# Reordering the work between the sub-layers of a two-layer diffusion trunk: where partial sums are taken, where conditioning products stand, which engine scales the first row

## The chip, the cores and the metric

The kernel runs on one core of a Trainium2 chip. The metric is device time in microseconds of one execution. The kernel before takes 1449.47 us (median of 3 runs, 1449.01 to 1450.84). All times in this text are microseconds unless marked otherwise.

A core has a matrix engine (PE, whose weight loads are listed as PEld), a vector engine (DVE), an activation engine (ACT), a general engine (POOL) and a queue engine that issues transfers (SP). Each runs its own instruction stream in order, and they wait for each other through semaphores.

## The reference

Two layers over 128 context tokens and 256 latent tokens of width 1024. Each layer has two sub-layers, a mixer and a convolutional feed-forward network, and each sub-layer has the same frame:

```python
for layer in range(2):
    mod = silu(cond) @ mod_w[layer] + mod_b[layer]          # six vectors of 1024, for context and for latents
    h = rmsnorm(x, w_pre) * (1 + mod[1]) + mod[0]           # pre-norm, shift and scale
    o = mixer(h)                                            # layer 0: SSD + DeltaNet; layer 1: gating MLP + attention
    x = x + mod[2] * rmsnorm(o, w_post)                     # post-norm, gate, residual
    h = rmsnorm(x, w_pre2) * (1 + mod[4]) + mod[3]
    o = (silu(a) * b) @ w_down                              # a, b = split(conv3(h @ w_up))
    x = x + mod[5] * rmsnorm(o, w_post2)
```

So between two sub-layers stands a serial stretch: the last output tile of `o` gives a sum of squares over 1024 features per token, its inverse root scales `o`, that updates `x`, a second inverse root scales `x`, and only then can the first matmul of the next sub-layer start. There are three such stretches inside the kernel and one at its end.

## The kernel before

**Layout.** Features lie on the 128 partitions, in 8 rows of tiles; tokens lie along the free axis (386 columns: 128 context tokens, a gap of 2, 256 latent tokens). A projection takes a 128x1024 block of weights per output tile. The weights come as 32-bit floats and are split into a high part (`whi`, a cast on ACT, L345) and a low part (`wlo`, a subtraction on DVE, L348); activations are split in the same way (`hh`, L371; `hl`, L372). Every product is three matmuls of 386 columns: high by high, low by high, high by low.

**Weights in order.** `plan` holds the list of all weight blocks. `fetch` takes the next one: a transfer of 512 KB from SP into one of 3 `wst` buffers (L339), then the split of its two halves of 512 columns into 6 `whi` and 6 `wlo` buffers. `wload` keeps two blocks ahead.

**Conditioning products.** `mod` is computed in 12 quads per layer (`quad`). A quad is five steps: four steps that each bring 512 KB of `mod_w` (L297) and do 8 small products on PE (L301; the profile counts 16 instructions for them, since each runs as two passes), and a fifth that copies the result on ACT (L305), transposes it on PE (L308) and adds the bias on DVE (L310). Its accumulator is one of the four PSUM buffers that the projections use too. Quads are placed in three ways: mixed one by one into the fill of a mixer (`weave`, with the quads' weights in the `wst` buffers), one step per index of the feed-forward network's loop (`early`, the constant `Q5`), or by `step(n)` between two sub-layers. The constants `S0`, `S1`, `S2` say how many steps are taken at three places there, by stretch (`gap` 0 after the layer 0 mixer, 1 after the layer 0 network, 2 after the layer 1 mixer). `Q2` and `Q4` say where the quads mixed into a mixer's fill end and those beside a residual begin. What is left is drained after the next pre-norm.

**Between two sub-layers.** `residual` takes the 8 output tiles. For each it squares the tile (L513), scales it into `u` by the gate (L508), squares that (L516) and multiplies it by `x` (L517): three partial products, added up over the tiles in `acc` (L520: the first on DVE, the two others on POOL). `colsum` (L498) turns such a tile into per-token means with three products of a single column (six instructions). In the kernel before, tiles 0 to 5 of the first sum and tile 6 of it are taken by `before`, called inside the last tile; the two other sums are taken after the last tile. Then `rsq` (an add on DVE, L409 or L411, and a power on POOL, L412) and `spread` (L420, six instructions on PE) give `r` and, by way of four small DVE instructions on `q` (L544 to L411), `r2`. After that `prenorms` goes through the 8 rows: `update` (`u*r` on DVE, L563; `x += u` on POOL, L564), `x*r2` on DVE (L471), shift and scale on ACT (L473, one instruction for context and one for latents), then the split into `hh` and `hl`. The first matmul group of the next sub-layer (`group`, L393 and L395) takes three output tiles at once, row by row, 9 matmuls per row.

**Order.** A scheduler that the kernel's language provides draws up each engine's stream at compile time, by the order of the program and by its own estimates of when an instruction is ready; a `with issue_after(ins)` block makes the instructions traced inside it follow `ins` on the engine of `ins`, and adds no wait between engines.

Of the kernel before, what the change touches and what calls it, by code (L numbers as in the profile page):

```python
# [27 lines left out]
S0, S1, S2 = [1, 2, 2], [9, 8, 4], [0, 0, 0]  # L28
# [207 lines left out]
class Net:  # L236
# [55 lines left out]
    def quad(self, l, q, pool):  # L292
        nc = self.nc
        acc = self.pmm.tile([128, 256], F32, name="pmod", tag="mm")
        for j in range(4):
            w = pool.tile([128, 1024], F32, name="wmod", tag="wst" if pool is self.wst else "wmod")
            nc.sync.dma_start(out=w, in_=self.t[f"modw_l{l}"][4 * q + j])  # L297
            for k in (2 * j, 2 * j + 1):
                for c in range(4):
                    o = 512 * (k % 2) + 128 * c  # L300
                    nc.tensor.matmul(acc[32 * c:32 * c + 32, 0:128], self.cond[:, k, :], w[:, o:o + 128],  # L301
                                     start=(k == 0), stop=(k == 7), tile_position=(0, 32 * c))
# [22 lines left out]
    def plan(self, seq):  # L325
        self.seq, self.ready, self.help, self.gap = list(seq), [], False, -1
# [8 lines left out]
    def fetch(self, after):  # L335
# [4 lines left out]
        parts = []  # L340
        for o in range(0, n, 512):
            m = min(512, n - o)
            hi, lo = (self.spare(n) or p.tile([128, 512], F32R, name=n, tag=n) for n, p in (("whi", self.whi), ("wlo", self.wlo)))
            with self.follow(after and after[0]):
                self.conv_hi = nc.scalar.copy(out=hi[:, 0:m], in_=st[:, o:o + m])  # L345
            eng = nc.gpsimd if o and self.help else nc.vector
            with self.follow(after and after[1]):
                self.conv_lo = eng.tensor_sub(out=lo[:, 0:m], in0=st[:, o:o + m], in1=hi[:, 0:m].bitcast(F32))  # L348
            parts.append((hi, lo))
        self.ready.append((src, parts))  # L350
# [9 lines left out]
    def prefetch(self, n, after=None):  # L360
        while len(self.ready) < n and self.seq:
            self.fetch(after)
# [7 lines left out]
    def split(self, hi, lo, src, eng=None):  # L370
        self.nc.scalar.copy(out=hi, in_=src)  # L371
        (eng or self.nc.vector).tensor_sub(out=lo, in0=src, in1=hi.bitcast(F32))  # L372
# [79 lines left out]
    def prenorms(self, l, nm, slot, r, hp, update=None, mods=None):  # L452
# [7 lines left out]
        step = 8 if mods is None else 2  # L460
        for k in range(8):
# [14 lines left out]
            if update:  # L476
# [1325 lines left out]
```

## Time and profile before

| | us |
|---|---|
| median of 3 runs | 1449.47 |
| the profiled execution's own time | 1449.51 |
| its span, first to last instruction | 1447.7 |
| PE busy | 1379.6 (95%) |
| DVE busy | 956.8 (66%) |
| ACT busy | 792.7 (55%) |
| POOL busy | 198.4 (14%) |

The span is what the views of the trace show; 1.8 us lie around it. PE is counted busy where a matmul is under way, and matmuls overlap, so busy time is not time at full rate. The profile also lists the clock that PE was granted, as a share of 2.4 GHz: 1.00, or 0.50 for 1.2 GHz, and a number between the two for a stretch that holds both.

### The profile page before, as it was taken

Reading aid. Unit: us, or ns where it says so; the run is one execution under the profiler, and the core shown is the slowest. Engines: PE = TensorE matmul, PEld = TensorE weight load, DVE = VectorE, ACT = ScalarE, POOL = GpSimd, SP = SyncE. Lnnn points to the kernel's source line nnn. Section 1 sums busy time; section 2 is a strip of 40 time slices with the busy share of each in tenths; the row PEclk is TensorE's granted clock in tenths of the full one; section 3 lists DMA queues with packets and bytes.
Section 4 is the critical chain, followed back from the end, with each engine's and each line's share of the span. In section 5 each row is a group of like instructions: output and inputs, shape, how many; then the busy total and the mean of one; then the engine's idle time right before and its main releaser. Section 6 shows DMA issues by size and latency. Waiting matters only on the chain.

```text
span 1447.7 us, 26153 instructions
## 1 busy us (share of the span) xinstructions
PE 1379.6 (95%) x10133; PEld 1306.4 (90%) x10133; DVE 956.8 (66%) x1879; ACT 792.7 (55%) x1749; POOL 198.4 (14%) x186
## 2 busy tenths in 40 slices
PE   5999998999998999999999999999999999999996
PEld 3889887999987789899999998999999899999996
DVE  3586999855989766676666445566567486767432
ACT  3578665668585436555455444544855465555341
POOL 0023110012355304200000113000002300000001
PEclk9999999999999999899999999999999999999998
DMA  9334544412643474545543442544234334343441
GB/s 347 130 101 142 174 138 143 142 42 79 199 161 117 139 238 170 210 154 162 170 134 114 128 126 74 160 146 134 83 117 153 125 117 131 117 131 115 128 126 55
DMA packets 60332, 201.58 MB, mean 139 GB/s; under 512 B 7120, under 2 KB 12000, under 8 KB 60208
## 3 DMA queue, kind: packets, MB, share of 16 engines
q1 hardware_dynamic: 52832, 186.25, 40.1%
q10 hardware_dynamic: 6048, 8.93, 1.7%
q0 software_dynamic: 1328, 4.73, 1.1%
q8 instruction: 80, 1.31, 0.4%
q14 instruction: 44, 0.36, 0.1%
HBM read 191.20 MB, written 8.68 MB: 138 GB/s over the span
## 4 chain that ended last, share of the span: by engine, by line
PE 79%; DVE 11%; issue 3%; ACT 3%; POOL 3%; DMA 1%; POOLq 0%; SPq 0%; ACTq 0%; DVEq 0%
PE mm L393 19%; PE mm L378 11%; PE mm L379 11%; PE mm L380 11%; PE mm L395 9%; PE pmod L301 3%; DVE wlo L348 2%; PE ps L498 1%; DVE t L700 1%; PE ps L1625 1%; PE mmt L1550 1%; PE mmt L1551 1%; PE mmt L1552 1%; DVE er L1133 1%; POOL er L809 1%
## 5 line engine op out<-in xcount | busy, mean ns | idle before, releaser
L348 DVE TENSOR_TENSOR wlo<-wst,whi 128x512 fp32r<-128x512 f32 (+1 forms) x497 | 344.2, 699 | 189.0 <-ACT whi L345 185.0
L345 ACT CAST whi<-wst 128x512 fp32r<-128x512 f32 (+1 forms) x505 | 304.2, 612 | 282.9 <-PE mm L379 151.2
L393 PE MATMUL mm<-hh,whi 128*128 128x386 f32 x728 | 247.7, 340 | 5.8 <-ACT hh L371 4.9
L393 PE MATMUL mm<-hh,wlo 128*128 128x386 f32 x728 | 245.9, 338 | 0.0
L395 PE MATMUL mm<-hl,whi 128*128 128x386 f32 x728 | 239.6, 340 | 0.3
L378 PE MATMUL mm<-hh,whi 128*128 128x386 f32 x552 | 198.0, 359 | 4.7 <-ACT t L1341 2.8
L380 PE MATMUL mm<-hh,wlo 128*128 128x386 f32 x552 | 191.6, 347 | 0.6 <-DVE wlo L348 0.6
L379 PE MATMUL mm<-hl,whi 128*128 128x386 f32 x552 | 191.9, 348 | 0.0
L393 PEld LDWEIGHTS mm<-hh,whi 128*128 128x128 f32 x728 | 137.1, 188 | 8.6 <-ACT hh L371 5.8
L395 PEld LDWEIGHTS mm<-hl,whi 128*128 128x128 f32 x728 | 136.1, 188 | 1.5 <-DVE hl L372 1.4
L393 PEld LDWEIGHTS mm<-hh,wlo 128*128 128x128 f32 x728 | 137.3, 189 | 0.0
L378 PE MATMUL mm<-gh,whi 128*128 128x386 f32 x352 | 119.5, 339 | 0.0
L379 PE MATMUL mm<-gl,whi 128*128 128x386 f32 x352 | 119.2, 339 | 0.0
L380 PE MATMUL mm<-gh,wlo 128*128 128x386 f32 x352 | 118.9, 338 | 0.0
L378 PEld LDWEIGHTS mm<-hh,whi 128*128 128x128 f32 x552 | 107.5, 195 | 11.9 <-issue 6.1
L598 DVE SCALAR_TENSOR_TENSOR t<-mm,vecs,t 128x385 f32<-128x385 f32 x88 | 54.3, 618 | 87.1 <-ACT t L597 87.1
L379 PEld LDWEIGHTS mm<-hl,whi 128*128 128x128 f32 x552 | 107.4, 195 | 0.7 <-issue 0.2
L380 PEld LDWEIGHTS mm<-hh,wlo 128*128 128x128 f32 x552 | 106.5, 193 | 1.0 <-DVE wlo L348 0.9
L700 DVE SCALAR_TENSOR_TENSOR t<-mm,vecs,t 128x384 f32<-128x384 f32 (+1 forms) x152 | 92.7, 613 | 12.3 <-ACT t L694 8.1
L597 ACT ACTIVATE t<-mm,vecs 128x386 f32<-128x386 f32 x88 | 58.9, 674 | 72.4 <-PE mm L395 72.4
L520 POOL TENSOR_TENSOR sums<-sums,t 128x386 f32<-128x386 f32 x36 | 41.5, 1175 | 337.6 <-DVE t L517 281.4
L301 PE MATMUL pmod<-wmod,cond 128*32 128x128 f32 x1536 | 67.2, 297 | 0.3 <-issue 0.3
(423 smaller groups left out, 2589.9 us busy)
## 6 DMA issues: line engine op xcount, KB each, us to landing
wmod<-modw_l SPq DMA_DIRECT2D x96, 512.0 KB, 4.4
wst<-up_l SPq DMA_DIRECT2D x88, 512.0 KB, 3.5
wst<-w SPq DMA_DIRECT2D x56, 512.0 KB, 4.0
wst<-wo SPq DMA_DIRECT2D x32, 512.0 KB, 3.9
wst<-down_l SPq DMA_DIRECT2D x32, 512.0 KB, 3.6
wst<-w1f SPq DMA_DIRECT2D x18, 512.0 KB, 3.6
wst<-down_l SPq DMA_DIRECT2D x16, 384.0 KB, 3.2
wst<-w1t SPq DMA_DIRECT2D x10, 512.0 KB, 3.6
```

The source lines that it names most:

```text
L301: nc.tensor.matmul(acc[32 * c:32 * c + 32, 0:128], self.cond[:, k, :], w[:, o:o + 128], start=(k == 0), stop=(k == 7), tile_position=(0, 3 ...
L345: self.conv_hi = nc.scalar.copy(out=hi[:, 0:m], in_=st[:, o:o + m])
L348: self.conv_lo = eng.tensor_sub(out=lo[:, 0:m], in0=st[:, o:o + m], in1=hi[:, 0:m].bitcast(F32))
L378: mm(ps, wh, xh, start=start, stop=False)
L379: mm(ps, wh, xl, start=False, stop=False)
L380: return mm(ps, wl, xh, start=False, stop=stop)
L393: mm(ps, w[k // 4][p][:, s], hh[:, k, :], start=(k == 0 and p == 0), stop=False)
L395: mm(ps, w[k // 4][0][:, s], hl[:, k, :], start=False, stop=(k == 7))
L520: (nc.gpsimd if i else v).tensor_add(out=acc[:, i, :], in0=acc[:, i, :], in1=p)
L597: nc.scalar.activation(out=cv, in_=ps, func=AF.Identity, scale=cw(1), bias=self.v(f"ffb_l{l}", n))
L598: stt(out=cv[:, 1:T], in0=ps[:, 0:T - 1], scalar=cw(0), in1=cv[:, 1:T], op0=ALU.mult, op1=ALU.add)
L700: nc.vector.scalar_tensor_tensor(out=o, in0=p, scalar=cw(i), in1=o, op0=ALU.mult, op1=ALU.add)
```

## The change

- `before` takes all three sums of `acc` inside the last tile. Tile 6 is added to `acc` for all three sums in stretches 1 and 2 (and for the one sum of the last residual); in stretch 0 (`direct`) tile 6 is not added at all, its products go to `colsum` one by one. `before` is called earlier in the last tile of both feed-forward networks (from row 16 to row 14 of 22) and of the layer 0 mixer (from row 5 to row 4 of 8), and later in that of the layer 1 mixer (from the start of its second half to the middle of it).
- The next weight block is fetched, and its first half split, right after the last tile; its second half is split behind the `hh` cast and the `hl` subtraction of row 0. Before, both halves followed the square of tile 7 (on ACT) and the first root (on DVE).
- Conditioning steps: one before the sum of tile 7's squares, two behind the last sum (`hold`), one behind `r2`: 4 in each stretch, where there were 10, 10 and 6. In exchange quad 1 of layer 1 moves into the layer 0 mixer's fill (`Q2`), six more steps into the layer 0 network's loop (`Q5`), and quad 10 into the layer 1 mixer's fill (`Q4`). `quad` now yields its fourth step before the ACT copy.
- Row 0: `x += u` moves from POOL to DVE, and the latents' shift and scale move from ACT to DVE (`first`). `x*r2` of rows 1 to 7 and `u*r` of rows 2 to 7 are queued behind `first` on DVE.

```diff
-S0, S1, S2 = [1, 2, 2], [9, 8, 4], [0, 0, 0]
+S0, S1, S2 = [1, 1, 1], [2, 2, 2], [1, 1, 1]
...
+            with self.follow(self.hold):
+                for k in (2 * j, 2 * j + 1):
...
-            if j == 3:
-                s = self.t386()[:, 0:128]
-                nc.scalar.copy(out=s, in_=acc[:, 0:128])
             yield 0.45
+        s = self.t386()[:, 0:128]
+        nc.scalar.copy(out=s, in_=acc[:, 0:128])
...
+        self.rest = self.halves(st, n, parts)
+        if halves:
+            next(self.rest)
+        else:
+            drain(self.rest)
...
             if update:
-                update(k)
-            nc.vector.tensor_mul(out=h, in0=self.x[:, k, :], in1=r)
+                with self.follow(first and k > 1 and first.ins):
+                    update(k)
+            with self.follow(first and first.ins):
+                nc.vector.tensor_mul(out=h, in0=self.x[:, k, :], in1=r)
             for s, (b, e) in enumerate(SEGS):
+                if update and k == 0 and s:
+                    first = nc.vector.tensor_scalar(out=h[:, b:e], in0=h[:, b:e], scalar1=a[:, k, s:s + 1],
+                                                    scalar2=m[:, k, 0, s:s + 1], op0=ALU.mult, op1=ALU.add)
+                    continue
...
-            self.split(hh[:, k, :], hl[:, k, :], h)
+            cast, cut = self.split(hh[:, k, :], hl[:, k, :], h)
+            if update and k == 0:
+                with self.follow(cast.ins), self.follow(cut.ins):
+                    drain(self.rest)
...
+        direct = self.gap == 0
+
         def before():
-            colsum(0, acc[:, 0, :], True)
-            colsum(0, part[0], False)
+            for i in range(num):
+                colsum(i, acc[:, i, :], i == 0)
+            if direct:
+                colsum(0, part[0], False)
...
-            if n:
-                for i, p in list(enumerate(part))[n // 6:]:
+            if 0 < n < 7 - direct:
+                for i, p in enumerate(part):
...
         o = out_tile(7, before)
+        if not last:
+            self.fetch(1)
+        if direct:
+            colsum(2, six[2], False)
...
-            colsum(2, acc[:, 2, :], True)
+            self.step(S0[self.gap])
         colsum(0, part[0], False)
...
-            colsum(1, acc[:, 1, :], True)
+            if direct:
+                colsum(1, six[1], False)
...
-            self.step(S0[self.gap])
+            self.hold = tail.ins
+            self.step(S2[self.gap])
             r2 = self.spread(rt2)
             self.step(S1[self.gap])
-            self.prefetch(3, (sq.ins, self.roots[0]))
+            self.hold = None
...
-                eng.tensor_add(out=self.x[:, n, :], in0=self.x[:, n, :], in1=u[:, n, :])
+                (eng if n else v).tensor_add(out=self.x[:, n, :], in0=self.x[:, n, :], in1=u[:, n, :])
...
-                    if mid and k0 + k == 16:
+                    if mid and k0 + k == 14:
...
-Q2 = 1
+Q2 = 2
 Q0 = 0
 Q3 = 8
-Q4 = 10
-Q5 = 15
+Q4 = 11
+Q5 = 21
...
-                if mid and k == 5:
+                if mid and k == 4:
...
+                w = net.wload(src(n, i))
+                half(ps, w, i, *x, range(4))
                 if mid and i:
                     mid()
-                half(ps, net.wload(src(n, i)), i, *x)
+                half(ps, w, i, *x, range(4, 8))
```

(Of S1 and S2 the roles change too: `S2` was a number of steps per row of the pre-norm, and now is the number taken behind the last sum.)

## Rows read from the trace of the kernel before

**Rows 1.** The page, busy time of PE: us, share, instructions.

```profile
PE 1379.6 (95%) x10133; PEld 1306.4 (90%) x10133; DVE 956.8 (66%) x1879; ACT 792.7 (55%) x1749; POOL 198.4 (14%) x186
```

**Rows 2.** Windows by stage: window, length, busy time by engine, PE clock, DMA share.

```profile
569.30:574.59 5.29, 4.10 (x23) 3.57 (x22) 2.81 (x4) 2.44 (x6) 3.54 (x4) 0.81 0.44 161
574.59:593.75 19.16, 17.07 (x172) 14.57 (x172) 6.82 (x21) 5.14 (x14) 6.10 (x7) 0.61 0.52 182
...
884.16:897.86 13.70, 11.38 (x172) 9.48 (x172) 6.80 (x21) 5.22 (x14) 6.04 (x6) 0.88 0.14 40
897.86:911.27 13.41, 13.28 (x74) 12.87 (x75) 10.10 (x19) 10.49 (x24) 4.97 (x6) 1.00 0.22 64
1136.96:1150.83 13.87, 11.73 (x155) 9.69 (x154) 5.84 (x17) 4.98 (x13) 4.58 (x5) 0.75 0.52 190
1150.83:1166.09 15.26, 14.06 (x89) 13.03 (x90) 12.69 (x23) 11.25 (x25) 6.45 (x7) 1.00 0.04 9
```

**Rows 3.** Timeline of PE, stretch 1: start, length, engine, line, operands, count, idle before.

```profile
885.97 1.50 PE L301 MATMUL pmod<-wmod,cond 128*32 128x128 f32 x42
887.40 0.83 PE L498 MATMUL ps<-cst,sums 128*128 128x1 f32 x6
888.09 1.48 PE L498 MATMUL ps<-cst,t 128*128 128x1 f32 x12
889.43 1.09 PE L420 MATMUL ps<-cst,rsq 128*128 128x130 f32 x6
...
891.80 1.65 PE L420 MATMUL ps<-cst,rsq 128*128 128x130 f32 x6 [0.29 <-POOL rsq L412]
...
897.86 0.44 PE L393 MATMUL mm<-hh,whi 128*128 128x386 f32 x1 [1.65 <-ACT hh L371]
```

**Rows 4.** Timeline of DVE, stretch 1.

```profile
885.47 0.62 DVE L530 TENSOR_TENSOR t<-mm,t 128x128 f32<-128x128 f32 x2 [4.63 <-ACT t L508]
...
889.68 0.16 DVE L544 TENSOR_TENSOR q<-ps,rsq 128x3 f32<-128x3 f32 x1 [3.44 <-PE ps L498]
...
890.34 0.69 DVE L348 TENSOR_TENSOR wlo<-wst,whi 128x512 fp32r<-128x512 f32 x1
...
891.63 0.55 DVE L563 TENSOR_TENSOR u<-u,ps 128x386 f32<-128x386 f32 x1
893.66 0.17 DVE L310 TENSOR_TENSOR mod<-pmod,vecs 128x8 f32<-128x8 f32 x1 [1.49 <-PE pmod L308]
893.74 1.48 DVE L563 TENSOR_TENSOR u<-u,ps 128x386 f32<-128x386 f32 x3
895.14 0.55 DVE L471 TENSOR_TENSOR t<-xres,ps 128x386 f32<-128x386 f32 x1
```

**Rows 5.** Timeline of ACT, stretch 1.

```profile
884.25 0.49 ACT L526 ACTIVATE t<-mm 128x386 f32<-128x386 f32 x1 [4.13 <-PE mm L380]
...
895.79 1.61 ACT L473 ACTIVATE t<-t,mod,ma 128x128 f32<-128x128 f32 x3
897.31 0.50 ACT L371 CAST hh<-t 128x386 fp32r<-128x386 f32 x1
```

**Rows 6.** Timeline of POOL, stretch 1.

```profile
890.50 1.24 POOL L412 TENSOR_TENSOR rsq<-rsq,mhalf 128x3 f32<-128x3 f32 x1 [3.33 <-DVE rsq L411]
892.25 1.00 POOL L564 TENSOR_TENSOR xres<-xres,u 128x386 f32<-128x386 f32 x1 [0.51 <-DVE u L563]
```

**Rows 7.** Windows of both networks' up halves, conditioning products (L301) alone: PE, PEld busy.

```profile
593.75:789.40 195.65, 7.11 (x192) 4.69 (x192) 1.00 0.48 153
1150.83:1339.90 189.07, 0.65 (x16) 0.38 (x16) 1.00 0.38 118
```

**Rows 8.** Timeline of PE, last tile of the layer 0 mixer.

```profile
571.22 0.83 PE L498 MATMUL ps<-cst,t 128*128 128x1 f32 x6 [1.19 <-ACT t L513]
```

**Rows 9.** Timeline of POOL, the same tile: two of the sums of tile 5.

```profile
568.30 2.70 POOL L520 TENSOR_TENSOR sums<-sums,t 128x386 f32<-128x386 f32 x2 [0.32 <-ACT t L516]
```

**Rows 10.** Timeline of PE, first matmul group after stretch 2: the transpose of a quad.

```profile
1162.61 0.33 PE L308 MATMUL pmod<-cst,t 128*128 128x128 f32 x1 [1.14 <-ACT t L305]
```

More of the change, by code (lines that the diff above doesn't have):

```diff
@@ L297, in quad @@
             nc.sync.dma_start(out=w, in_=self.t[f"modw_l{l}"][4 * q + j])
[L298 to L302, printed above, removed]
-            if j == 3:
-                s = self.t386()[:, 0:128]
-                nc.scalar.copy(out=s, in_=acc[:, 0:128])
+            with self.follow(self.hold):
+                for k in (2 * j, 2 * j + 1):
+                    for c in range(4):
+                        o = 512 * (k % 2) + 128 * c
+                        nc.tensor.matmul(acc[32 * c:32 * c + 32, 0:128], self.cond[:, k, :], w[:, o:o + 128],
+                                         start=(k == 0), stop=(k == 7), tile_position=(0, 32 * c))
             yield 0.45
+        s = self.t386()[:, 0:128]
+        nc.scalar.copy(out=s, in_=acc[:, 0:128])
         tr = acc[:, 128:256]
@@ L325, in plan @@
     def plan(self, seq):
-        self.seq, self.ready, self.help, self.gap = list(seq), [], False, -1
+        self.seq, self.ready, self.help, self.gap, self.hold = list(seq), [], False, -1, None
         self.more = {"whi": 0, "wlo": 0}
@@ L333, in spare, with fetch @@
         return self.extra.tile([128, 512], F32R, name=name, tag=name, bufs=MORE)
-    def fetch(self, after):
+    def fetch(self, halves=0):
         nc = self.nc
@@ L340, in fetch, with halves @@
         parts = []
+        self.ready.append((src, parts))
+        self.rest = self.halves(st, n, parts)
[3 more added lines that the diff above has]
+            drain(self.rest)
+    def halves(self, st, n, parts):
+        nc = self.nc
         for o in range(0, n, 512):
@@ L343, in fetch @@
             hi, lo = (self.spare(n) or p.tile([128, 512], F32R, name=n, tag=n) for n, p in (("whi", self.whi), ("wlo", self.wlo)))
-            with self.follow(after and after[0]):
-                self.conv_hi = nc.scalar.copy(out=hi[:, 0:m], in_=st[:, o:o + m])
+            self.conv_hi = nc.scalar.copy(out=hi[:, 0:m], in_=st[:, o:o + m])
             eng = nc.gpsimd if o and self.help else nc.vector
-            with self.follow(after and after[1]):
-                self.conv_lo = eng.tensor_sub(out=lo[:, 0:m], in0=st[:, o:o + m], in1=hi[:, 0:m].bitcast(F32))
+            self.conv_lo = eng.tensor_sub(out=lo[:, 0:m], in0=st[:, o:o + m], in1=hi[:, 0:m].bitcast(F32))
             parts.append((hi, lo))
-        self.ready.append((src, parts))
+            yield
     @contextmanager
@@ L358, in follow, with prefetch @@
         return self.tc.issue_after(ins) if ins else nullcontext()
-    def prefetch(self, n, after=None):
+    def prefetch(self, n):
         while len(self.ready) < n and self.seq:
-            self.fetch(after)
+            self.fetch()
     def wload(self, src, ahead=2):
@@ L370, in split @@
     def split(self, hi, lo, src, eng=None):
-        self.nc.scalar.copy(out=hi, in_=src)
-        (eng or self.nc.vector).tensor_sub(out=lo, in0=src, in1=hi.bitcast(F32))
+        return (self.nc.scalar.copy(out=hi, in_=src),
+                (eng or self.nc.vector).tensor_sub(out=lo, in0=src, in1=hi.bitcast(F32)))
     def acc(self, ps, w, k, xh, xl, start, stop):
@@ L460, in prenorms @@
         step = 8 if mods is None else 2
+        first = None
         for k in range(8):
@@ L523, in residual @@
             scaled(gx, self.x[:, 7, :], 7, AF.Copy)
+        six = part
         o = out_tile(7, before)
+        if not last:
+            self.fetch(1)
+        if direct:
+            colsum(2, six[2], False)
         part = [self.t386() for i in range(num)]
```

2 lines of the change are left out of this document (removed).

## The prediction

> **What bounds the kernel now.** I read the page first. PE is busy 95% of the span [rows 1], so most stages are bound by PE, and an edit pays only where PE waits or does something that need not be on the path. Then the windows by stage: the three stretches between sub-layers, from the end of the last tile's last matmul to the first matmul of the next group, take 19.16, 13.70 and 13.87, and the clock granted in them is 0.61, 0.88 and 0.75, while it is 1.00 in the matmul groups behind them [rows 2]. That is 46.7 in sum in which no projection runs. Last the timelines of stretch 1, engine by engine, which show what its 13.70 consist of:
>
> - PE does 42 conditioning instructions (885.97) before it takes the 18 instructions of the sums that `q` needs (887.40 to 889.43); `q` starts at 889.68, late by those 42 [rows 3, 4].
> - The power on POOL takes 1.24, the spread of `r2` 1.65 and ends at 893.45 [rows 3, 6].
> - `x*r2` of row 0 could start there, but starts at 895.14: ahead of it on DVE stand two halves of `wlo`, the bias of a quad, which waits 1.49 for PE's transpose, and `u*r` of three more rows, 1.48 [rows 4].
> - ACT then scales (row 0's two instructions among three, 1.61) and casts 0.50; PE starts at 897.86 after 1.65 idle [rows 3, 5].
>
> So each stretch is a chain of latencies, and PE's conditioning work in it is a filler that lies partly on the chain.
>
> **The stretch after the change, step by step** (times from the end of the last tile, durations from stretch 1). The square on ACT starts at 0.09 [rows 5]; the product with `x` on DVE ends at 1.93 (886.09 less 884.16) [rows 4]. PE takes one conditioning step (16 instructions at 1.43/42 = 0.034, so 0.55) and the sum of squares (six instructions, 2.03/18 x 6 = 0.68) in that time [rows 3]. The other twelve instructions follow at 1.93 and end at 3.3. `q` starts 0.25 later as now, four DVE instructions bring POOL's power to 4.4 (889.68 to 890.50 is 0.82), it ends at 5.6, and `r2`'s spread ends at 7.3 [rows 3, 4, 6]. `r` is spread from 3.4 to 4.5, so `u*r` of row 0 (0.49, a third of 1.48) and `x += u` are done by 5.6, and two conditioning steps fit on PE in front of `r2`. `x*r2` takes 0.5 to 7.9, ACT's scaling 0.5 (half of the pair), the cast 0.5, and PE starts at 8.9. The splits of weights and the later rows are no longer in front.
>
> Three edits cost nothing on that path, as long as their cover holds. `x += u` of row 0 on DVE is not in the trace; it lies between the DVE product of the same shape, 0.49, and POOL's 1.00 [rows 4, 6]; I take 0.49, and either ends before `r2` is there (without that cover, up to 1.0). The latents' scaling on DVE lies between 0.16 (three columns) and 0.55 (386 columns) [rows 4]; I take 0.35, beside ACT's 0.5. The first half of the next block is split within the last tile, whose matmuls hide it; the second half stands on ACT behind the cast of row 0 and ahead of row 1's scaling (0.6 there), on DVE behind row 0's `hl` (0.69 [rows 4]).
>
> **Per stretch.**
> - Stretch 1: 13.70 to 8.9 is -4.8. Inside the last tile stand 18 sum instructions in place of 12, +0.7. The group behind it, now 13.41 for 8 rows [rows 2], loses a head start: four rows had `u*r` done when it began, now two have. After stretch 2, where the head start is two rows, the group keeps PE's pace but for conditioning work, so I add 0.5 (bounds 0 and 3: a row needs 1.5 of DVE and 1.0 to 1.35 of POOL [rows 6, 9] against 1.68 of PE). One transpose of a quad comes behind the pre-norm, +0.3. Sum -3.3.
> - Stretch 2: 13.87 to 8.9, +0.7. The group takes 15.26 [rows 2], for it holds one conditioning step and PE waits 1.14 before a quad's transpose [rows 10]; I take 14.2, as one transpose remains. Sum -5.4.
> - Stretch 0 is the odd one. In the last tile PE waits 1.19 for the square of tile 6 [rows 8], and POOL finishes tile 5's sums only at 571.0 (568.30 + 2.70) [rows 9]. `before` now stands a row earlier and wants POOL's sums too, so PE reaches the wait about 0.5 sooner; the twelve extra instructions fit partly into it. I take +0.9 on the end of the tile (0 to 1.7). The clock falls around this wait (0.81 from 569.30 to 574.59, 0.61 behind it [rows 2]). Behind the tile stand 30 sum instructions as before. At 2.4 GHz the path is 8.9 + 0.85 = 9.75 (two more sums of six, 1.36, of which 0.5 falls into a wait). At 1.2 GHz the 30 sums and `r2`'s spread take twice their time: + 3.4 + 1.65 = 14.8. I take the middle, 12.2: -7.0. The group +0.5. Sum -5.6.
> - The stretch at the end: one sum of six fewer in its last tile, -0.7.
>
> **What leaves the stretches comes back elsewhere.** They did 128, 128 and 112 + 16 conditioning instructions; they now do 64 each: 12 product steps and 4 transposes move into matmul-bound stages. Their price shows in the two networks: layer 0's up half takes 195.65 with 192 such instructions (12 steps), layer 1's 189.07 with 16 [rows 7]. Without that step and the waiting transpose (0.6 + 1.4) layer 1's is 187.0, so 12 steps and their 3 transposes cost 8.6, 0.72 a step. So +8.6 for the 12 moved ones. Their transfers (12 of 512 KB) go to queues that stand at a DMA share of 0.38 to 0.48 in those halves [rows 7] and are hidden; in the two mixers they take `wst` buffers from the weights, which I bound by twice the price for those 8 steps, +5.8, and by zero, if the mixers' chains leave PE idle there.
>
> **The clock behind the stretches.** Rows 2 show 0.88 and 0.75 in stretches 1 and 2, and 1.00 in the groups: now the low clock ends before the group, under the conditioning products. With fewer of them it may reach into the group; I put 0.8 on it for both. The Trainium skill, "TensorE: Matmul & The Clock Gate", Part 1, speaks against the change here: PE's clock is throttled by default and activity releases it, so a filler that looks like waste may be what keeps the group fast. By that rule alone the first rival below would be the likely case; the trace bears it out only so far as the clock is 0.61 to 0.88 in the stretches and 1.00 behind them, with fillers present.
>
> **Sum.** -3.3 - 5.4 - 5.6 - 0.7 + 8.6 + 0.8 = -5.6. The profiled execution's own time is 1449.51, at the median of the runs (1449.47), so the forecast is 1443.9.
>
> **Rivals.**
> - *The clock stays low into the groups* (slower). From the last sums on, PE runs at 1.2 GHz: twelve sum instructions (+1.35), `r2`'s spread (+1.65) and the first row of the group (+1.7) cost 4.7 per stretch, 14.1 for three, less 0.8 and 2.5 that the sum holds already: +10.8, 1454.7. It decides from 3.0 per stretch on. For it: the clock in stretch 0 stays at half for most of 19 with 128 fillers. Against: stretch 1 recovers within it. Chance 0.12.
> - *The rows become the bound.* Row by row the chain DVE, POOL, DVE, ACT runs behind PE, or the scheduler sets other work ahead of row 0 again, so that the change doesn't do what it says; the three groups lengthen by 2.0 and not by 0.5: +4.5, 1448.4. For it: the head start is gone, and rows 2 to 7 are queued behind `first`. Against: the group after stretch 2. Chance 0.20.
> - *The moved products cost double in the mixers*: +5.8, 1449.7. Chance 0.10.
> - *Stretch 0 keeps its clock*: 9.75 in place of 12.2, no later tile, no low clock in the groups: -2.5 - 0.9 - 0.8, 1439.7. Chance 0.16.
>
> **How the numbers follow.** The forecast has 0.42, with its own range 1441 to 1447. Any single measurement of this kernel separates about 0.2%, 2.9. Faster by more than that: the forecast nearly whole (0.38), the full-clock case 0.16, some of the two near-unchanged cases 0.06, so 0.60. Slower by more: the clock case 0.10 and the doubled price's far end 0.02, so 0.12. The rest, 0.28, is no change. The range 1438.5 to 1450.5 leaves out the clock case and the far ends of the full-clock and doubled-price cases.
>
> **What would show it.** Right: stretches 1 and 2 near 8.9, `q` within 4 of the last tile's end, `x*r2` of row 0 directly behind the spread of `r2`, no `wlo` before it; layer 0's up half near 199; one more quad in each mixer at about 2.9. Wrong: a stretch over 11, groups over 15, a clock under 1.00 in the groups' windows, PE waiting over 2 in the last tile of the layer 0 mixer, or a mixer longer by over 5.

## The result, and the profile after

The kernel after takes 1462.68 us (median of 4 runs, 1459.46 to 1464.32), against 1449.24 for the kernel before on the same chip: 1.0095 times, interval 1.0076 to 1.0114. It is slower by 13.4 where 5.6 faster was forecast, and lies outside the range. The profiled execution took 1464.1, its span is 1462.0.

One slip in the text ahead of the prediction changes no sum: in the kernel after one conditioning step stands behind the last sum and two behind the spread of `r2`, not two and one.

The page, busy time of PE, as in [rows 1]:

```profile
PE 1383.2 (95%) x10127; PEld 1297.6 (89%) x10127; DVE 963.8 (66%) x1888; ACT 792.9 (54%) x1746; POOL 192.2 (13%) x181
```

PE is busy 3.6 longer in a span that is 14.3 longer; the rest is idle time. The windows by stage, which answer to [rows 2]: last tile, stretch and first group (eight rows, 72 matmuls) of stretch 0, then stretch and group of 1 and 2.

```profile
579.28:585.36 6.08, 5.48 (x32) 5.40 (x32) 3.18 (x5) 2.94 (x7) 1.37 (x1) 0.82 0.36 123
585.36:598.80 13.44, 12.47 (x107) 10.91 (x106) 4.64 (x15) 2.91 (x8) 3.03 (x4) 0.57 0.25 80
598.80:618.76 19.96, 15.34 (x74) 12.38 (x74) 16.28 (x29) 14.92 (x32) 6.91 (x6) 1.00 0.35 109
...
899.97:909.42 9.45, 8.10 (x94) 6.42 (x95) 4.83 (x16) 2.91 (x8) 2.96 (x3) 0.82 0.11 42
909.42:924.88 15.46, 13.19 (x64) 10.85 (x65) 12.75 (x23) 11.16 (x24) 7.01 (x8) 1.00 0.19 63
1157.74:1165.81 8.07, 6.62 (x95) 5.27 (x95) 4.69 (x15) 2.91 (x8) 3.04 (x4) 1.00 0.01 2
1165.81:1182.87 17.06, 14.85 (x74) 12.49 (x75) 14.03 (x26) 12.24 (x27) 6.91 (x6) 1.00 0.12 42
```

The stretches fell as forecast: 19.16 to 13.44, 13.70 to 9.45, 13.87 to 8.07, together -15.8 (forecast -16.8). The groups behind them rose: counted to the next matmul behind their 72 they took 16.08, 13.25 and 15.27 before and take 19.96, 15.46 and 17.06 now, at a clock of 1.00. (The 16.08 ends with conditioning instructions and a wait, 2.84 in all; the groups of the kernel after hold no conditioning step.) PE is busy 15.34 of 19.96. What holds it shows in stretch 2. First PE:

```profile
1157.67 0.65 PE L302 MATMUL pmod<-wmod,cond 128*32 128x128 f32 x16
1158.38 0.83 PE L513 MATMUL ps<-cst,t 128*128 128x1 f32 x6
1159.73 1.50 PE L513 MATMUL ps<-cst,t 128*128 128x1 f32 x12 [0.52 <-DVE rsq L416]
...
1163.07 0.94 PE L427 MATMUL ps<-cst,rsq 128*128 128x130 f32 x6
...
1165.81 0.44 PE L400 MATMUL mm<-hh,whi 128*128 128x386 f32 x1 [0.79 <-ACT hh L378]
...
1167.77 0.45 PE L400 MATMUL mm<-hh,whi 128*128 128x386 f32 x1
...
1170.05 0.45 PE L400 MATMUL mm<-hh,whi 128*128 128x386 f32 x1 [0.35 <-ACT hh L378]
...
1172.60 0.44 PE L400 MATMUL mm<-hh,whi 128*128 128x386 f32 x1
```

The chain to 1165.81 is the one that was drawn up; the first rows then start 1.96, 2.28 and 2.55 apart, where nine matmuls at PE's pace take 1.6. DVE, in the same time:

```profile
1161.34 0.16 DVE L569 TENSOR_TENSOR q<-ps,rsq 128x3 f32<-128x3 f32 x1 [1.66 <-PE ps L513]
...
1164.07 0.56 DVE L481 TENSOR_TENSOR t<-xres,ps 128x386 f32<-128x386 f32 x1
1164.66 0.42 DVE L484 TENSOR_SCALAR t<-t,ma,mod 128x256 f32<-128x256 f32 x1
...
1165.45 0.55 DVE L589 TENSOR_TENSOR u<-u,ps 128x386 f32<-128x386 f32 x1
1165.92 0.55 DVE L379 TENSOR_TENSOR hl<-t,hh 128x386 fp32r<-128x386 f32 x1
1166.39 1.51 DVE L355 TENSOR_TENSOR wlo<-wst,whi 128x512 fp32r<-128x512 f32 x1
...
1168.76 1.01 DVE L589 TENSOR_TENSOR u<-u,ps 128x386 f32<-128x386 f32 x2
1170.42 0.56 DVE L481 TENSOR_TENSOR t<-xres,ps 128x386 f32<-128x386 f32 x1 [0.65 <-POOL xres L590]
```

and POOL:

```profile
1166.08 1.27 POOL L590 TENSOR_TENSOR xres<-xres,u 128x386 f32<-128x386 f32 x1 [1.19 <-DVE u L589]
1169.38 1.98 POOL L590 TENSOR_TENSOR xres<-xres,u 128x386 f32<-128x386 f32 x2 [2.03 <-DVE u L589]
```

The second half of `wlo` stands between row 0 and row 1 and takes 1.51 beside POOL's addition (1.52 in the two other stretches), for 0.69 alone [rows 4]. `u*r` of row 2, queued behind `first` (L484), runs only at 1165.45, that of rows 3 and 4 at 1168.76, behind that `wlo`; POOL adds row 3 at 1169.38, and `x*r2` waits for it at 1170.42. So the rows are served by a DVE that is full and a POOL that is fed late. In stretch 0 a second wait follows the rows, that of PE for a quad's transpose, whose copy (L306) ACT takes behind the first outputs' work:

```profile
617.73 0.33 PE L308 MATMUL pmod<-cst,t 128*128 128x128 f32 x1 [1.65 <-ACT t L306]
618.76 0.44 PE L400 MATMUL mm<-hh,whi 128*128 128x386 f32 x1 [0.70 <-DVE t L626]
```

The rest of the loss lies mostly in stages that took up steps: layer 0 mixer +5.5 up to its last tile, layer 0 up half behind its group +6.2, layer 1 mixer +7.0 (0.7 of it the six more sum instructions in its last tile). Another +4.2 lies in the DeltaNet part of layer 0, which took up none.

### The profile page after: what moved, and what is told of

Same layout as the page of the kernel before. It is cut to its first block, busy times and chain, and to the rows that moved or that the text cites. A ratio compares the mean times of both kernels' runs of the same rounds, so it can differ in the third digit from the quotient of the medians.

```text
span 1462.0 us, 26143 instructions
## 1 busy us (share of the span) xinstructions
PE 1383.2 (95%) x10127; PEld 1297.6 (89%) x10127; DVE 963.8 (66%) x1888; ACT 792.9 (54%) x1746; POOL 192.2 (13%) x181
## 4 chain that ended last, share of the span: by engine, by line
PE 77%; DVE 11%; DMA 3%; issue 3%; ACT 3%; POOL 2%; SPq 0%; POOLq 0%; ACTq 0%; DVEq 0%
PE mm L400 18%; PE mm L385 11%; PE mm L386 10%; PE mm L387 10%; PE mm L402 9%; PE pmod L302 3%; DVE t L726 2%; DVE wlo L355 2%; PE ps L513 1%; PE mmt L1576 1%; PE ps L1651 1%; PE mmt L1577 1%; PE mmt L1578 1%; DVE er L835 1%; DVE u L589 1%
## 5 line engine op out<-in xcount | busy, mean ns | idle before, releaser
L726 DVE SCALAR_TENSOR_TENSOR t<-mm,vecs,t 128x384 f32<-128x384 f32 (+1 forms) x152 | 92.7, 612 | 13.5 <-ACT t L720 10.1
L385 PEld LDWEIGHTS mm<-gh,whi 128*128 128x128 f32 x352 | 66.5, 189 | 0.0
```

The costliest lines, as they stand in the source:

```text
L385: mm(ps, wh, xh, start=start, stop=False)
L726: nc.vector.scalar_tensor_tensor(out=o, in0=p, scalar=cw(i), in1=o, op0=ALU.mult, op1=ALU.add)
```

## The experiments

All ratios are to the kernel before on the same chip, with 95% intervals. Single runs of this kernel scatter by up to 7 either way, so verdicts rest on the ratios; profiles show where, not how much.

**One part alone on the kernel before.** The quad's copy (behind its fourth step's `yield`, as in the kernel after):

```diff
-            if j == 3:
-                s = self.t386()[:, 0:128]
-                nc.scalar.copy(out=s, in_=acc[:, 0:128])
             yield 0.45
+        s = self.t386()[:, 0:128]
+        nc.scalar.copy(out=s, in_=acc[:, 0:128])
```

> The kernel before with one edit alone: a quad's copy on ACT stands behind the fourth yield, next to its transpose. Layer 0's mixer is 3.9 longer in the changed kernel up to the end of its delta part, where no quad was added and no other edit reaches. Theory 'copy': the later copy makes PE wait at the transposes (10.6 in place of 7.0 over the kernel) and shifts the fill of the delta part: +3 to +6. Rival 'scatter of the schedule': the copy does nothing by itself (within 1.5 of before), and the 3.9 come from somewhere later in the program through the scheduler or from run to run.

Measured 1450.97, 1.0020 (1.0004 to 1.0037): about +2.9.

The moved steps, old copy:

```diff
-S0, S1, S2 = [1, 2, 2], [9, 8, 4], [0, 0, 0]
+S0, S1, S2 = [1, 1, 1], [3, 3, 3], [0, 0, 0]
...
-Q2 = 1
+Q2 = 2
...
-Q4 = 10
-Q5 = 15
+Q4 = 11
+Q5 = 21
```

> The kernel before with the placement of the conditioning steps alone changed: 4 steps in each stretch, quad 1 in the layer 0 mixer's fill, 21 steps in the layer 0 network's loop, quad 10 in the layer 1 mixer's fill. My forecast's terms: +8.6 in the bodies, and each stretch shorter by the six steps that are partly on its path, 2 to 3 each: about 1449. Theory 'moved work': the bodies pay 13 to 19 as in the changed kernel, so 1455 to 1460. Rival 'rows': within 3 of before.

Measured 1453.66, 1.0038 (1.0020 to 1.0057): about +5. In its profile the three stretches are 10.3 shorter than before, but the groups behind them run at a clock of 0.80 to 0.84, with PE busy throughout:

```profile
591.75:606.60 14.85, 14.85 (x72) 14.82 (x73) 12.60 (x22) 10.97 (x24) 6.30 (x7) 0.84 0.08 15
...
898.32:913.48 15.16, 15.16 (x72) 15.14 (x73) 11.62 (x21) 10.88 (x23) 6.31 (x8) 0.83 0.20 58
...
1153.42:1168.97 15.55, 15.55 (x73) 15.49 (x73) 12.74 (x23) 10.98 (x24) 6.32 (x7) 0.80 0.11 28
```

The sums:

```diff
         def before():
-            colsum(0, acc[:, 0, :], True)
-            colsum(0, part[0], False)
+            for i in range(num):
+                colsum(i, acc[:, i, :], i == 0)
+            if direct:
+                colsum(0, part[0], False)
...
-            if n:
-                for i, p in list(enumerate(part))[n // 6:]:
+            if 0 < n < 7 - direct:
+                for i, p in enumerate(part):
```

> The kernel before with the edits of the sums alone (three sums of tiles 0 to 6 inside the last tile, stretch 0's tile 6 by itself, the earlier or later call). Forecast's terms: the tail of the sums is 0.7 to 1.4 earlier in each stretch, the last tiles 0.7 to 0.9 longer, the last residual -0.7: within 2 of before. Rival 'sums': the sums are the loss, since PE waits in the layer 0 mixer's last tile and the clock falls there: +4 to +8.

Measured 1451.14, 1.0011 (0.9995 to 1.0027): nothing. The stretches shrank in its profile (15.49, 13.33, 11.81), but row 0 still stood behind the weights' splits and a quad's bias.

The weights' split:

```diff
         o = out_tile(7, before)
+        if not last:
+            self.fetch(1)
...
-            self.prefetch(3, (sq.ins, self.roots[0]))
...
+            if update and k == 0:
+                with self.follow(cast.ins), self.follow(cut.ins):
+                    drain(self.rest)
```

> The kernel before with the edits of the weight split alone (first half of the next block split within the last tile, second half behind row 0's cast and subtraction). Forecast: the two halves of wlo leave the front of row 0, 1.4 less on DVE, but DVE waits for a quad's transpose there anyway: -1 to 0 per stretch, -2 in sum. Rival 'split': the second half now costs 0.6 on ACT and 1.5 on DVE between row 0 and row 1 (in the changed kernel's trace it takes 1.51 there), and the weights come later: +1 to +2 per stretch, +3 to +6.

Measured 1443.32, 0.9952 (0.9934 to 0.9970): 6 faster than the kernel before, and faster than both kernels.

Row 0:

```diff
             if update:
-                update(k)
-            nc.vector.tensor_mul(out=h, in0=self.x[:, k, :], in1=r)
+                with self.follow(first and k > 1 and first.ins):
+                    update(k)
+            with self.follow(first and first.ins):
+                nc.vector.tensor_mul(out=h, in0=self.x[:, k, :], in1=r)
...
+                if update and k == 0 and s:
+                    first = nc.vector.tensor_scalar(out=h[:, b:e], in0=h[:, b:e], scalar1=a[:, k, s:s + 1],
...
-                eng.tensor_add(out=self.x[:, n, :], in0=self.x[:, n, :], in1=u[:, n, :])
+                (eng if n else v).tensor_add(out=self.x[:, n, :], in0=self.x[:, n, :], in1=u[:, n, :])
```

> The kernel before with the edits of row 0 alone (x += u and the latents' scaling on DVE, rows queued behind it). Forecast: row 0 is ready 1.0 to 2.0 earlier in each stretch, the group loses 0.5: -3 in sum. Rival 'rows': x*r2 of rows 1 to 3 and u*r of rows 2 and 3, which run before PE starts now, come behind row 0, and each of the three groups lengthens by 2 to 4: +3 to +6.

Measured 1450.06, 1.0002 (0.9986 to 1.0019): nothing. By medians the five effects (+1.9, +4.6, +1.8, -6.0, +0.7) add up to +3.0, where the whole change costs 13.4: parts collide.

**One part taken from the kernel after.** The counts of the steps as before, nearly at their old places (one stands ahead of the sums), the new copy and `hold` kept:

```diff
-S0, S1, S2 = [1, 1, 1], [2, 2, 2], [1, 1, 1]
+S0, S1, S2 = [1, 1, 1], [8, 8, 4], [1, 1, 1]
...
-Q2 = 2
+Q2 = 1
...
-Q4 = 11
-Q5 = 21
+Q4 = 10
+Q5 = 15
```

> The changed kernel with the conditioning products back in the three stretches (10, 10 and 6 steps there, 15 in the layer 0 network's loop, one quad less in each mixer's fill); sums, row 0, weight split and queueing stay changed. Theory 'moved work': reading the two traces, layer 0's mixer with its tiles is about 10 later at its last tile, layer 0's up half 6 longer beside its first group, layer 1's mixer 3 longer, 19 in sum, and putting the products back into the stretches costs them at most 12 x 0.55 = 6.6, so the time falls by 10 or more, to about 1450. Rival 'rows': the first groups behind the stretches (17.1, 17.0, 17.1 in place of 13.2, 13.4, 15.3) are the loss, they stay, and the time stays above 1457.

Measured 1461.92, 1.0090 (1.0061 to 1.0118): no different from the kernel after. Putting the steps back wins nothing by itself.

The queue behind `first`:

```diff
             if update:
-                with self.follow(first and k > 1 and first.ins):
-                    update(k)
-            with self.follow(first and first.ins):
-                nc.vector.tensor_mul(out=h, in0=self.x[:, k, :], in1=r)
+                update(k)
+            nc.vector.tensor_mul(out=h, in0=self.x[:, k, :], in1=r)
```

> The changed kernel without the queueing behind row 0's scaling on DVE (updates of rows 2 to 7 and x*r2 of rows 1 to 7 are free again). Theory 'queue': the queueing delays the update of rows 2 and up, and is why the three first groups take 17 each and not 13.5: without it groups shorten by 2 to 3 each and the stretches lengthen by 1 to 2, so 1456 to 1460. Rival 'head start': PE starts earlier than the rows can follow whatever their order, since a row takes DVE 1.5 to 2 and POOL 1.0 to 1.3 in a chain; the end of the group doesn't move, the time stays within 2 of the changed kernel.

Measured 1458.79 (1449.84 to 1462.78), 1.0086 (1.0056 to 1.0116): unclear. The profiled run is the lowest of the four; its groups of stretches 0 and 2 are 2.5 and 2.3 shorter than in the kernel after.

All of row 0's part (the queue as above, and):

```diff
-                if update and k == 0 and s:
-                    first = nc.vector.tensor_scalar(out=h[:, b:e], in0=h[:, b:e], scalar1=a[:, k, s:s + 1],
...
-                (eng if n else v).tensor_add(out=self.x[:, n, :], in0=self.x[:, n, :], in1=u[:, n, :])
+                eng.tensor_add(out=self.x[:, n, :], in0=self.x[:, n, :], in1=u[:, n, :])
```

> The changed kernel without the edits of row 0 (x += u on POOL and both scalings on ACT as before, no queueing). Theory 'rows': the groups shorten by 2 to 4 each and the stretches lengthen by 1: 1453 to 1458. Rival 'composite': no single part carries the loss; it stays above 1458, and the parts taken one by one add up to about 13 (moved steps measured at +4.6).

Measured 1456.69, 1.0050 (1.0031 to 1.0070): 6 less than the kernel after. Row 0's part costs nothing alone and 6 in company.

**Pairs on the kernel before.** Sums, split and row 0 (the three diffs above together):

```diff
+            for i in range(num):
+                colsum(i, acc[:, i, :], i == 0)
...
+            self.fetch(1)
...
+            with self.follow(first and first.ins):
```

> The kernel before with three parts, sums, weight split and row 0; conditioning steps, their order and the quad as before. Alone the three measured +1.8, -6.0 and +0.7. Theory 'sum of parts': about 1446. Rival 'interaction': the parts work against each other in the row pipeline, where the second half of the split (1.5 on DVE) now stands between row 0 and row 1 of a queued pipeline and the head start is gone: 1453 to 1460, near the 1461.9 of the changed kernel with the steps put back.

Measured 1451.84 (1446.40 to 1461.83), 1.0021 (0.9997 to 1.0045).

Sums and split:

```diff
+            for i in range(num):
+                colsum(i, acc[:, i, :], i == 0)
...
+            self.fetch(1)
```

> The kernel before with the sums and the weight split. Theory 'sum of parts': 1445. Rival 'interaction': q is ready earlier, so the rows start earlier with fewer of them updated, and the second half of the split falls among them: 1448 to 1453.

Measured 1447.76, 0.9984 (0.9962 to 1.0005): 4.4 above the split alone (the intervals just overlap), so the sums bring the split no gain; row 0's part costs some 4 on top (these intervals overlap too).

Split and row 0:

```diff
+            self.fetch(1)
...
+            with self.follow(first and first.ins):
```

> The kernel before with the weight split and the edits of row 0. Theory 'sum of parts': 1444. Rival 'interaction': the queue behind row 0 and the second half of the split meet on DVE and ACT in front of row 1, the groups lengthen by 2 or more each: 1449 to 1455.

Measured 1452.93, 1.0036 (1.0015 to 1.0056): 9.6 over the split alone. The collision needs these two parts only; the timeline of DVE in its first group has the rows of the kernel after again (L580 is POOL's addition):

```profile
593.75 1.53 DVE L355 TENSOR_TENSOR wlo<-wst,whi 128x512 fp32r<-128x512 f32 x1
...
597.81 0.56 DVE L481 TENSOR_TENSOR t<-xres,ps 128x386 f32<-128x386 f32 x1 [0.66 <-POOL xres L580]
```

In the split alone the second half stands at the same place, behind `hl` of row 0, and takes 0.69: there POOL has added its first rows by then and is idle until 591.75.

```profile
589.58 0.69 DVE L355 TENSOR_TENSOR wlo<-wst,whi 128x512 fp32r<-128x512 f32 x1
...
591.75 2.34 POOL L573 TENSOR_TENSOR xres<-xres,u 128x386 f32<-128x386 f32 x2 [3.91 <-DVE u L572]
```

Split, moved steps and the quad's late copy:

```diff
+            self.fetch(1)
...
+S0, S1, S2 = [1, 1, 1], [3, 3, 3], [0, 0, 0]
...
             yield 0.45
+        s = self.t386()[:, 0:128]
+        nc.scalar.copy(out=s, in_=acc[:, 0:128])
```

> The kernel before with the weight split, the quad's later copy, and the moved conditioning steps (4 in a stretch, the rest in the bodies), without the holds. Moved steps alone measured +4.6, the copy +1.9, the split -6.0. Theory 'sum of parts': about 1449.8. Rival 'interaction': with the filler gone the rows have no head start, and the second half of the split delays them: 1453 to 1458.

Measured 1463.97, 1.0105 (1.0082 to 1.0128): 20.6 over the split alone, a second collision.

**Which element.** The kernel after with both halves of the next block split in the last tile:

```diff
-            if update and k == 0:
-                with self.follow(cast.ins), self.follow(cut.ins):
-                    drain(self.rest)
...
-            self.fetch(1)
+            self.fetch()
```

> The kernel after with both halves of the next block split inside the last tile, none of it behind row 0. Theory (the second half between row 0 and row 1 stretches the groups): the first 73 matmuls of the network groups fall from 20 and 17 to 16 and 15, and the time from 1462.7 to 1455-1458. Rival (the queue behind first does it): the groups stay at 17 to 20 and the time within 2 of 1462.7.

Measured 1456.96, 1.0052 (1.0035 to 1.0069), below the kernel after's interval: the theory holds, -5.7. The groups of the two networks fell to 17.9 and 15.1 (16 and 15 were expected).

The kernel after with the old copy:

```diff
+            if j == 3:
+                s = self.t386()[:, 0:128]
+                nc.scalar.copy(out=s, in_=acc[:, 0:128])
             yield 0.45
-        s = self.t386()[:, 0:128]
-        nc.scalar.copy(out=s, in_=acc[:, 0:128])
```

> The kernel after with the quad's copy on ACT back in its fourth step, ahead of the yield. Theory (the late copy makes PE wait for the transpose, in the fills and in the group of stretch 0): PE's waits for the copy fall from 10.6 to about 7 over the kernel, the layer 0 network's up half loses 2 to 4, and the time is 1453 to 1458. Rival (the placement of the steps alone costs it): within 2 of 1462.7.

Measured 1459.66, 1.0078 (1.0059 to 1.0097): 3 lower, between the theory and the rival, and not separated from the kernel after. The wait for the transpose behind the first group is gone from its profile (19.96 to 17.01); the waits of PE and its weight loads for the copy fall from 10.6 to 5.8.

Split and row 0 without the queue:

```diff
+            self.fetch(1)
...
+                if update and k == 0 and s:
+                    first = nc.vector.tensor_scalar(out=h[:, b:e], in0=h[:, b:e], scalar1=a[:, k, s:s + 1],
...
+                (eng if n else v).tensor_add(out=self.x[:, n, :], in0=self.x[:, n, :], in1=u[:, n, :])
```

> The kernel before with the weight split part and with row 0's work on DVE (x += u and the latents' scaling), but rows 1 to 7 not queued behind it. Theory (the queue and the split's second half collide): no collision without the queue, so 1441 to 1444, no slower than the split alone (1443.3). Rival (row 0's work on DVE is itself late for the split): 1447 to 1453, as with the queue (1452.9).

Measured 1444.26, 0.9965 (0.9950 to 0.9979): the theory. Against split and row 0 with the queue (1.0036) the queue is worth 8.7 here, and the work of row 0 on DVE nothing.

Split and moved steps with the old copy:

```diff
+            self.fetch(1)
...
+S0, S1, S2 = [1, 1, 1], [3, 3, 3], [0, 0, 0]
...
-Q5 = 15
+Q5 = 21
```

> The kernel before with the weight split part and the moved conditioning steps, the quad's copy where it was before. Theory (the late copy made 1464.0 of it): 1448 to 1452, that is the split's -6 and the placement's +4.6 or the forecast +8.6. Rival (fewer steps in the stretches and the split are enough for the loss): 1459 to 1465, with low clock in and behind stretch 0.

Measured 1451.73, 1.0018 (1.0003 to 1.0033): the theory; the late copy makes 12.2 of the difference to the kernel with it (1463.97). Windows of stretch 0, its group and the rest of the up half show where most of it is, first with the late copy:

```profile
581.97:598.79 16.82, 14.11 (x107) 12.19 (x106) 5.16 (x15) 3.67 (x10) 4.66 (x6) 0.50 0.39 128
598.79:616.95 18.16, 15.81 (x73) 15.30 (x74) 15.17 (x27) 14.23 (x31) 6.08 (x7) 0.84 0.22 63
616.95:804.29 187.34, 187.34 (x1244) 179.44 (x1245) 123.01 (x215) 93.84 (x171) 0.00 (x0) 0.99 0.48 149
```

then with the old copy:

```profile
579.71:592.16 12.45, 8.68 (x107) 7.46 (x107) 5.67 (x15) 3.93 (x11) 5.18 (x6) 0.80 0.56 193
592.16:607.37 15.21, 15.21 (x72) 15.21 (x73) 12.93 (x23) 11.40 (x25) 6.12 (x7) 0.82 0.19 47
607.37:792.55 185.18, 185.18 (x1245) 177.86 (x1245) 125.57 (x218) 96.32 (x175) 0.00 (x0) 1.00 0.49 154
```

With the late copy the stretch is 4.4 longer and runs wholly at 1.2 GHz (0.50 against 0.80), the group is 3.0 and the rest of the up half 2.2 longer. Why the clock was lower there is not shown.

**All three taken back.** The kernel after with the whole split in the last tile, the old copy, and no queue (the diffs of those three runs together):

```diff
-            self.fetch(1)
+            self.fetch()
...
+            if j == 3:
+                s = self.t386()[:, 0:128]
+                nc.scalar.copy(out=s, in_=acc[:, 0:128])
...
-                with self.follow(first and k > 1 and first.ins):
-                    update(k)
+                update(k)
```

> The kernel after with three things taken back at once: both halves of the next block are split inside the last tile, the quad's copy is in its fourth step again, rows 1 to 7 are not queued behind row 0. Theory (these three are the loss, and they add up): 1462.7 less 5.7, 3.0 and 3.9 is 1450, and if pairs of them collided as in the smaller kernels, 1444 to 1448; the first 73 matmuls of the network groups at 14 to 16.5. Rival (the moved steps do not fit beside the other parts, whatever the three): 1453 to 1458, with the layer 0 network's up half and the layer 1 mixer still 6 and 6 longer than in the kernel before.

Measured 1449.18, 0.9996 (0.9982 to 1.0010): 13.5 less than the kernel after. The three together are the whole loss against the kernel before; the sums, the moved steps and row 0's work on DVE remain in this kernel. Whether each of the three is needed beside the two others is not shown. Its windows, stretch and group of stretches 0, 1 and 2:

```profile
583.24:597.70 14.46, 12.68 (x107) 10.94 (x106) 7.34 (x19) 3.69 (x11) 4.97 (x6) 0.61 0.39 118
597.70:612.02 14.32, 14.32 (x72) 14.32 (x73) 11.08 (x21) 10.66 (x24) 4.92 (x4) 0.88 0.24 91
892.61:902.72 10.11, 6.95 (x96) 5.41 (x96) 7.42 (x20) 4.05 (x11) 4.90 (x5) 1.00 0.25 88
902.72:915.96 13.24, 13.06 (x72) 12.74 (x73) 9.58 (x19) 10.03 (x22) 5.07 (x6) 1.00 0.20 57
1146.18:1156.73 10.55, 8.38 (x96) 6.45 (x96) 7.41 (x20) 3.73 (x11) 4.97 (x6) 0.84 0.17 51
1156.73:1170.01 13.28, 13.20 (x73) 12.67 (x74) 11.82 (x22) 10.89 (x24) 4.63 (x4) 1.00 0.03 4
```

DVE is busy 7.4 in each stretch, in place of 4.6 to 4.8, and less in the group. Its timeline in stretch 2 shows with what: `u*r` of two more rows ahead of `first` (L483) and `x*r2` of row 1 ahead of it and of two more just behind it, and the next `wlo` only in the sixth row.

```profile
1152.75 1.02 DVE L585 TENSOR_TENSOR u<-u,ps 128x386 f32<-128x386 f32 x2
1153.93 1.02 DVE L480 TENSOR_TENSOR t<-xres,ps 128x386 f32<-128x386 f32 x2 [0.17 <-PE ps L428]
1154.88 0.96 DVE L483 TENSOR_SCALAR t<-t,ma,mod 128x256 f32<-128x256 f32 x1
1155.75 1.01 DVE L480 TENSOR_TENSOR t<-xres,ps 128x386 f32<-128x386 f32 x2
...
1158.01 1.25 DVE L380 TENSOR_TENSOR hl<-t,hh 128x386 fp32r<-128x386 f32 x1 [0.27 <-ACT hh L379]
...
1165.72 0.68 DVE L356 TENSOR_TENSOR wlo<-wst,whi 128x512 fp32r<-128x512 f32 x1
```

That is later for row 0 (the stretches are 1.0, 0.7 and 2.5 longer) and earlier for the rows behind it: the groups are 5.6, 2.2 and 3.8 shorter and run at PE's pace, 13.3 (14.3 where the clock is 0.88). Over three stretches the queue, the second half and the copy win 4.2 ahead of the group and lose 11.6 in it. Against the kernel before, the stretches and groups of this one are 15.4 shorter in its profile, and all other stages together 16.7 longer, 12.0 of it in the mixers and up halves, where the steps went. So the gain of the stretches is spent there.

The same with the steps where the kernel before has them:

```diff
-S0, S1, S2 = [1, 1, 1], [2, 2, 2], [1, 1, 1]
+S0, S1, S2 = [1, 2, 2], [9, 8, 4], [0, 0, 0]
...
-            self.hold = tail.ins
-            self.step(S2[self.gap])
+            self.step(S0[self.gap])
...
-Q5 = 21
+Q5 = 15
```

> The cured kernel (whole split in the last tile, quad's copy in the fourth step, no queue behind row 0) with the conditioning steps of the kernel before (10, 10 and 6 in the stretches, none moved). Theory (moving costs more in the mixers and the network than the stretches give back): the layer 0 network's up half and the layer 1 mixer are again 5 to 6 and 3 to 5 shorter, the stretches 2 to 4 longer each, and the time is 1440 to 1445. Rival (the steps' work is the same wherever it stands): 1447 to 1451, no different from 1449.2.

Measured 1448.29 (1439.38 to 1451.75), 0.9993 (0.9975 to 1.0011): the rival; in this company moving the steps neither wins nor loses. In the profiled runs (the one here is 8.9 below its kernel's median) the three stretches sum to 35.3 with 344 instructions of the products in them, those of the kernel above to 35.1 with 184: there a step costs a stretch nearly nothing. But 96 more of these instructions, six steps, stand in the groups here, which sum to 46.3 in place of 40.8.

## Why the prediction was wrong

The profiled executions, forecast against measured; the measured differences sum to 14.3, the spans' difference.

| | forecast | measured |
|---|---|---|
| three stretches | -16.8 | -15.8 |
| last tiles, the residual at the end | +1.6 | +1.8 |
| first groups behind the stretches | +0.2 | +7.9 |
| moved steps in mixers and up halves | +8.6 | +16.1 |
| low clock in groups | +0.8 | 0 |
| layer 0's DeltaNet part, the end | 0 | +4.3 |

**Right.** The chain of each stretch: `q` stands 3.6 behind the last tile's end in stretches 1 and 2 (7.8 in stretch 0, at a clock of 0.57), `x*r2` directly behind the spread of `r2`, and no `wlo` between. Stretch 2 came out under 8.9 by two sizes: the power took 0.85 and not 1.24, the spread of `r2` 0.94 and not 1.65, at a clock of 1.00. The tile of the layer 0 mixer cost 1.07 (0.9), the last residual gave 0.64 (0.7).

**The step that failed: "the group keeps PE's pace but for conditioning work, so I add 0.5 (bounds 0 and 3)".** It was read off the group after stretch 2 of the kernel before, "where the head start is two rows". That reading mixes two counts. When that group began, at 1150.83, `x*r2` of two rows was done, but `u*r` of four, as many as after stretch 1; the two of the kernel after are counted in `u*r`. DVE of the kernel before:

```profile
1146.59 1.01 DVE L563 TENSOR_TENSOR u<-u,ps 128x386 f32<-128x386 f32 x2
1148.27 0.56 DVE L471 TENSOR_TENSOR t<-xres,ps 128x386 f32<-128x386 f32 x1 [0.66 <-POOL xres L564]
1149.23 0.56 DVE L471 TENSOR_TENSOR t<-xres,ps 128x386 f32<-128x386 f32 x1 [0.41 <-POOL xres L564]
1149.70 1.01 DVE L563 TENSOR_TENSOR u<-u,ps 128x386 f32<-128x386 f32 x2
```

Nor did a half of a `wlo` stand between rows 0 and 1 there (the next ran at 1160.89), and `u*r` and `x*r2` were not queued: DVE did later rows' work ahead of the group. I counted the second half as 0.69 and then gave it no cost; it took 1.51, as it falls on POOL's addition. The rival "the rows become the bound", with "rows 2 to 7 are queued behind `first`" for its reason, was the case (chance 0.20), and at 2.0 a group it was still too small: the groups exceed the 13.3 of PE's pace by 6.7, 2.2 and 3.8, 2.8 of the first being the transpose and the waits around it. That the queue and the second half need each other is shown by the split and row 0 parts alone and together, and by the two together without the queue; that these two and the copy together are all of the loss against the kernel before, by the kernel without them.

**The copy.** I added 0.3 for "one transpose of a quad" behind one pre-norm. With `yield` ahead of the copy, ACT takes it behind other work; with the split and moved steps it cost 12, most of it in the stretch, the group and the up half, the stretch at a lower clock; taken out of the kernel after it gave 3, not separated from nothing. A change of one line's place was not priced as a moved instruction.

**The moved steps.** 0.72 a step is right for the network: behind the group of the kernel without the three causes, layer 0's up half holds 128 more instructions of the products (eight steps, since PE does none of them in the group) and is 5.6 longer, 0.70 each, and the whole half took 199.5 ("near 199"). In the mixers, where I had 0.72 with a bound of twice that, it is more: in that same kernel the layer 0 mixer is 4.6 longer and the layer 1 mixer 3.7, their last tiles apart, 8.3 for 5.8 forecast. The kernel after pays 11.8 there, the bound; of the excess of 3.5 I can't say more than that it went with the three causes. In the runs' times the price doesn't show: where the steps were they cost some 5.5 in the groups, and what makes up the rest is open.

**The clock.** The rival in which it stays low into the groups is not borne out in the kernel after: 1.00 in all three groups, 0.57, 0.82 and 1.00 in the stretches, 63 of the span at 1.2 GHz in the profiled run against 73 before. It is what the profile of the moved steps alone shows: groups at 0.80 to 0.84, 5.7 in sum above PE's pace of 13.3 each. So the rival was no idle one, and which of the other edits keeps the clock up in the kernel after is not shown.

**Open.** +4.2 in the DeltaNet part of layer 0, where of the edits only the quad's later copy reaches, is not explained: that part ends at 442.0 before and at 446.3 after, and between 441.3 and 445.6 in the other kernels' profiles, with either copy.

## What to carry to other kernels

Shortening a serial stretch by queueing everything behind its first result moves the queued work into the stage that follows; price that stage's stream on the engine that feeds it, instruction by instruction, for the first few rows, before the stretch's gain is counted. Work that fills an engine's wait is free only there: in the stretches the further conditioning steps cost nearly nothing, in the groups some 0.9 each, and in the mixers the moved ones about 1.0. Parts that cost 0 to 3 alone can cost 9 and 12 in company, and a part of a losing change can win: the split of the next weights, half in the last tile and half behind row 0, gives 0.9952 alone.

## What the runs showed of the hardware

- A DVE subtraction with both inputs in SBUF takes longer beside a POOL addition: `wlo` 1.51 to 1.53 for 0.69, `hl` 1.25 for 0.55 in the kernel without the three causes, while `x*r2` and `u*r`, with one input in PSUM, stay at 0.5 to 0.56. The Trainium skill, "SBUF — State Buffer", "Who interferes with whom", says that a DVE instruction with two SBUF inputs contends with a POOL instruction that reads SBUF; this trace agrees (1166.39 on DVE, 1166.08 to 1167.35 on POOL).
- Runs of one kernel differ in the clock granted on average, and their times go with it: over 126 runs of the kernel before it lies between 0.972 and 0.982, the time between 1442.85 and 1456.61 (medians 1452.6 at 0.974 and 1445.1 at 0.981, correlation -0.77). The split alone had 0.9805 in the median, the split with steps and late copy 0.967, the kernel before beside them 0.977 and 0.976: by the slope of 0.9 per 0.001, an estimate, some 3 of the former's 6 and some 8 of the latter's 15 go with the clock. Whether the clock is the cause there or follows from PE's waits is not shown.
